# Key norms' sums behind the receptance tile and the low-rank products, the gates' small weights in program order on VectorE, two operations of each key tile on ScalarE

## The chip, the cores and the metric

The kernel runs on one core of one Trainium2 chip. The metric is the time of one execution on the device in microseconds (us). The engines are named as the profile names them: PE (matrix products), DVE (vector engine), ACT (scalar engine), POOL (GpSimd) and SP, which only issues transfers. Each engine works through its own queue in order, and waits where an instruction needs a result of another engine that isn't there yet.

## The reference, cut to what matters

One layer of a hybrid trunk on 512 frames of 1024 values, all in float32: a gated convolution, an RG-LRU and an RWKV-7 mixer, merged by gates, then an output projection and a squared-ReLU MLP.

```python
h = rms_norm(x, norm1_g)
p = h @ w_in                                   # 1024 -> 11520 columns
pa, pb, pg, pc = _split(p, (COLS_A, COLS_B, COLS_GATE, COLS_C))
y_a = b_a * causal_dwconv(c_a * x_a, conv_a_w)
y_b = rg_lru(causal_dwconv(x_b, lru_conv_w, lru_conv_b), ...) * gelu(g_b)
...
pc = token_shift(pc, rwkv_mu)                  # p + (prev - p) * mu
r, k, v, xw, xa, xg = _split(pc, (D_C, D_C, D_C, R_W, R_A, R_G))
decay = exp(-exp(-softplus(-(w0 + tanh(xw) @ w2)) - 0.5))
a = sigmoid(a0 + xa @ a2)
g_c = sigmoid(xg) @ g2
kk = heads(k * k_k)
kk = kk / maximum(sqrt(sum(kk * kk, axis=-1, keepdims=True)), 1e-12)
k = k * (1.0 + (a - 1.0) * k_a)
yc = rwkv7_recurrence(r, decay, k, v, kk, a)   # chunks of 64 frames
...
m = gate_a * y_a + gate_b * y_b + gate_c * y_c
x = x + m @ w_out
x = x + square(relu(rms_norm(x) @ mlp_w1)) @ mlp_w2
return rms_norm(x, final_g)
```

The change touches the lines of `kk` (the norm of each head's keys), `decay`, `a` and the second `k` line, and in the gates the product with `g2`.

## The kernel before

**Products.** All large products are float32 made of two parts: an operand is cast to a high part and the rest is subtracted (`hi`, `lo`), and a product takes three matmuls (`mm3`, L168 to L170). A projection tile has 128 output columns and 512 frames, so 8 x 3 = 24 matmuls of 128x512 into one PSUM bank of the pool `pp` (three banks). Its weights come by one transfer on SP (`raw`, two buffers), one cast on ACT (`whi`, L147) and one subtraction on DVE (`wlo`, L104), three buffers each. Everything smaller shares the two banks of the pool `pm`: the key sums `pn`, the low-rank products `pw` and `pa`, and the inverse's `pG` and `pT` among others.

**The key tiles.** `krv(g)` makes keys, receptance and values of group g; there are four groups and two key tiles j in each, eight in all. A key tile does this: the k projection and its token shift (`shift`, ACT L325 then DVE, gives `ks`); a square of the scaled keys on ACT (L430), split into `bh` and `bl` (L163 and L104); the sum over each head as two matmuls with a block matrix `bd` into `pn` (L433, L434); the root `rsqrt_rows`, which transposes (L194, tile `rqw`), works in 11 small steps on `rqq` and transposes back (L201); and `kk`, one DVE product of that with `ks`. Then the r projection and its shift (`rs`); the small weights `swa` (cast on ACT and subtraction on DVE, L406 and L104); `pw` (L444, L445), Tanh on ACT into `sig` (L447), plus one on DVE (L448); `pa` (L450, L451) and its Tanh into `av` (L453); the running sum of `sig` (`cum`, L455) and two Exp of it on ACT (L459, L462); and from all these the operands of the recurrence, `AR` and `BK`. There `kp` is one DVE operation with two scalars (L469, shown in the profile as L110, the line of the helper `ts2`), times `ks`. `ks`, `rs`, `kk` and the other work tiles of a key tile have one buffer each, so the next key tile's writes wait for this one's last reads.

**What runs beside them.** Of the previous group, `inverse(g-1)` inverts 64x64 triangular blocks: 31 steps of two DVE operations on tiles `dg` and `Z`, then transposes (L573, L578), 32 small matmuls `pG` (L585), and 32 more, `pT` (L595). `ab(q)` (the convolution and RG-LRU work, eight q) fills in everywhere. After the last inverse come the chain over the eight chunks with the gates beside it (`gate(q)`, small weights `swc`), the output projection and the MLP.

**What sets the order.** The code is written as generators, which `weave` runs alternately, so many steps of the filling work to one step of the critical one; a `yield` is the place where the other one may go on. A tile scheduler then orders each engine's queue by the priorities that `tc.high_priority` gives and by its own estimate of when things are ready; `tc.keep_in_program_order` holds one instruction where the program has it. The lines that the change touches are in `krv` and in `load_sw`:

```python
pn = pm.tile([P, S], F32, tag="pm", name="pn")
pe.matmul(pn, bd, sqh, start=True, stop=False)
pe.matmul(pn, bd, sql, start=False, stop=True)
kk = WP("a5")
rsqrt_rows(pk, kk, pn, 1e-24)
stt(kk, ks, pv("kk", j), kk, MUL, MUL)
```

Of the kernel before, what the change touches and what calls it, by code (L numbers as in the profile page):

```python
# [9 lines left out]
F32 = mybir.dt.float32  # L10
F32R = mybir.dt.float32r
I32 = mybir.dt.int32
AF = mybir.ActivationFunctionType
# [5 lines left out]
P = 128  # L19
# [14 lines left out]
S = 512  # L34
# [64 lines left out]
def block_kernel(ctx, tc, xt, win, par, mulr, sw, wout, w1, w2, fg, cst, eyes, out):  # L99
# [3 lines left out]
    def tt(o, a, b, op):  # L103
        return v.tensor_tensor(out=o, in0=a, in1=b, op=op)  # L104
# [9 lines left out]
    def f(t):  # L114
        return t.bitcast(F32)
# [135 lines left out]
    for i in range(2):  # L251
        load_half(wlr[1], win[CN[("lr", 1)]], i)
    gp.memset(epst[:, 0:1], EPS)
    wu = pc.tile([P, S], F32, tag="pu", name="wu")
    for i in range(NWARM):
        pe.matmul(wu, ones, zer, start=True, stop=True)
# [67 lines left out]
    def shift(pt, mu, omu, o):  # L324
        ac.activation(o, pt, AF.Copy, scale=omu)  # L325
        stt(o[:, 1:], pt[:, 0:S - 1], mu, o[:, 1:], MUL, ADD)
# [8 lines left out]
    def WP(tag, bufs=1):  # L335
        return pk.tile([P, S], F32, tag=tag, name=tag, bufs=bufs)
# [64 lines left out]
    def load_sw(pool, tag, j, a, n):  # L401
        raw = wp.tile([P, 2, P], F32, tag="swr", name="swr", bufs=2)
        sy.dma_start(raw[:, 0:n], sw[j, :, a:a + n])
        hi = pool.tile([P, n, P], F32R, tag=tag + "h", name=tag + "h", bufs=1)
        lo = pool.tile([P, n, P], F32R, tag=tag + "l", name=tag + "l", bufs=1)
        ac.copy(hi, raw[:, 0:n])  # L406
        tt(lo, raw[:, 0:n], f(hi), SUB)
        return hi, lo

    def c3(t):  # L410
# [5 lines left out]
    def krv(g, G_):  # L416
        G_.AR = pk.tile([P, 2, NC, 2, L], F32, tag="AR", name="AR")
        G_.BK = pk.tile([P, 2, NC, 2, L], F32, tag="BK", name="BK")
        vs = [p1.tile([P, S], F32, tag=f"v{h}", name=f"v{h}") for h in range(2)]
        for jj in range(2):  # L420
            j = 2 * g + jj
            rs = WP("rs")
            if j == 0:
                ks = k0
            else:
                ks = WP("ks")
                t = yield from proj(("k", j))
                shift(t, pv("mu_k", j), dvp(OMK, j), ks)
            sq = WP("a1")
            ac.activation(sq, ks, AF.Square, scale=pv("kk", j))  # L430
            sqh, sql = split(pk, sq, "b")
            pn = pm.tile([P, S], F32, tag="pm", name="pn")
            pe.matmul(pn, bd, sqh, start=True, stop=False)  # L433
            pe.matmul(pn, bd, sql, start=False, stop=True)  # L434
            kk = WP("a5")
            rsqrt_rows(pk, kk, pn, 1e-24)
            stt(kk, ks, pv("kk", j), kk, MUL, MUL)
            yield
            t = yield from proj(("r", j))
            shift(t, pv("mu_r", j), dvp(OMR, j), rs)  # L440
            yield
            swh, swl = load_sw(pk, "swa", j, 0, 2)
            pw = pm.tile([P, S], F32, tag="pm", name="pw")
            pe.matmul(pw, swh[:, 0], lws, start=True, stop=False)  # L444
            pe.matmul(pw, swl[:, 0], lws, start=False, stop=True)  # L445
            sig = WP("a1")
            ac.activation(sig, pw, AF.Tanh, bias=pv("w0", j), scale=0.5)  # L447
            v.tensor_scalar(out=sig, in0=sig, scalar1=1.0, scalar2=None, op0=ADD)  # L448
            pa = pm.tile([P, S], F32, tag="pm", name="pa")
            pe.matmul(pa, swh[:, 1], las, start=True, stop=False)  # L450
            pe.matmul(pa, swl[:, 1], las, start=False, stop=True)  # L451
            av = WP("a4")
            ac.activation(av, pa, AF.Tanh, bias=pv("a0", j), scale=0.5)  # L453
            cum = WP("a2")
            v.tensor_tensor_scan(out=cum, data0=smk, data1=sig, initial=0.0, op0=MUL, op1=ADD)  # L455
            PP = pk.tile([P, NC, L + 1], F32, tag="PPt", name="PPt")
            gp.memset(PP[:, :, 0:1], 1.0)
            Pt = PP[:, :, 1:L + 1]
            ac.activation(Pt, c3(cum), AF.Exp, scale=-0.5 * CW)  # L459
            v.tensor_copy(PL[:, g, jj], PP[:, :, L])  # L460
            pinv = WP("a3")
            ac.activation(pinv, cum, AF.Exp, scale=0.5 * CW)  # L462
            stt(G_.AR[:, jj, :, 0], c3(kk), -1.0, PP[:, :, 0:L], MUL, MUL)
            tt(G_.AR[:, jj, :, 1], c3(rs), Pt, MUL)
            t_ = WP("a1")
            stt(t_, av, 1.0, kk, ADD, MUL)
            stt(G_.BK[:, jj, :, 0], c3(t_), 0.5, c3(pinv), MUL, MUL)
            kp = WP("a2")
            ts2(kp, av, pv("ka", j), dvp(OKA, j), MUL, ADD)  # L469
            tt(kp, kp, ks, MUL)  # L470
            tt(G_.BK[:, jj, :, 1], c3(kp), c3(pinv), MUL)

            if jj == 0:
                rk = [WP(f"rk{h}") for h in range(2)]
            for h in range(2):
                r = slice(64 * h, 64 * h + 64)
                stt(rk[h][64 * jj:64 * jj + 64], rs[r], part[r, PI["rk"], j:j + 1], kp[r], MUL, MUL)

        for jj in range(2):
            for h in range(2):  # L480
                gp.dma_start(axd[:, 0:64, g, 0, 2 * h + jj].rearrange("c d t -> d c t"),
                             G_.AR[64 * h:64 * h + 64, jj, :, 0])
            gp.dma_start(rtd[:, :, g, jj].rearrange("c p t -> p c t"), G_.AR[:, jj, :, 1])
        rk = [split(pk, rk[h], ("a1", "a3") if h else "b") for h in range(2)]
        for h in range(2):
            q = 2 * g + h
            t = yield from proj(("v", q))
            shift(t, pv("mu_v", q), dvp(OMV, q), vs[h])
            yield
        for h in range(2):  # L490
            pb = pm.tile([P, S], F32, tag="pm", name="pb")
            for i in range(2):
                pe.matmul(pb, bd, rk[h][i], start=i == 0, stop=i == 1)
            BV[2 * g + h] = [bv_tile(2 * g + h, th) for th in range(2)]
            for th in range(2):
                tt(BV[2 * g + h][th], pb[:, HALF[th]], vs[h][:, HALF[th]], MUL)
        yield
        for b in range(2):
            pt = pm.tile([P, 2, 2, P], F32, tag="pm", name="pV")
            for i in range(2):  # L500
                for h in range(2):
                    pe.transpose(pt[:, i, h], vs[h][:, (2 * b + i) * P:(2 * b + i + 1) * P], ident)
            vt = p1.tile([P, 2, 2, P], F32, tag="vt", name="vt", bufs=2)
            ac.copy(vt, pt)
            for i in range(2):
                c = 2 * (2 * b + i)
                gp.dma_start(vtd[c:c + 2, :, g].rearrange("c s e v -> (c s) (e v)"),
                             vt[:, i].rearrange("p h x -> p (h x)"))
        yield
# [619 lines left out]
```

## Time and profile before

| what | us |
|---|---|
| median of three runs | 1109.31 |
| lowest and highest of them | 1108.31, 1109.75 |
| the profiled execution | 1108.38 |
| its span, first to last instruction | 1106.6 |
| PE idle in the span (1106.6 - 1056.1) | 50.5 |

The rows of the profile are read so. A group's row gives line, engine, operation, `out<-in`, shapes and count, then the busy time in us and the mean of one in ns, then the idle time of the engine just before and what ended it. A row of waits gives the engine and line that waited, the engine and line that it waited for, the total in us, the count and the longest. A row of windows gives the stretch, its length, each engine's busy us with the number of instructions (PE, then PEld, DVE, ACT and POOL where all are shown), then the clock granted to PE as a share of full speed, the DMA share and GB/s. A row of the timeline gives start and duration in us, and in brackets the idle time before it with what ended it.

By time the program falls into: the prologue (0 to 49), the key tiles with the inverses and the filling work (49 to 560), the chain with the gates (560 to 715), then output projection and MLP.

### The profile page before, as it was taken

The numbers are of one execution on the slowest core, as the hardware profiler recorded it, in microseconds if no ns is written. First come the engines' busy times: TensorE is split into PE (matmuls) and PEld (weight loads), VectorE is DVE, ScalarE is ACT, GpSimd is POOL, SyncE is SP. The second block draws the span as 40 slices with busy tenths as digits, with TensorE's granted clock in tenths as the row PEclk, the third lists the DMA queues.
The fourth block names the chain that finished last, engine by engine and source line by source line (L and its number), as shares of the span: only waits on it lengthen the run. The fifth ranks groups of instructions, "written<-read, shape, count | busy, mean of one in ns | idle before, by whom it ended". The sixth has DMA issues, their size and how long they took to land.

```text
span 1106.6 us, 16112 instructions
## 1 busy us (share of the span) xinstructions
PE 1056.1 (95%) x6396; PEld 865.3 (78%) x6396; DVE 743.6 (67%) x1276; ACT 473.9 (43%) x698; POOL 108.9 (10%) x167
## 2 busy tenths in 40 slices
PE   8899979999799989999899999999999999999996
PEld 5677868887588867887687887898888888888885
DVE  7997898879978998769947677955444443222224
ACT  6655445454344534534555444334433333221114
POOL 3211000210011101210022220001000000000001
PEclk9899989999989989999999999999999999999999
DMA  6243623562234623553279773234333335322231
GB/s 209 83 124 98 180 79 113 139 182 86 77 105 129 177 85 96 147 148 106 79 225 281 263 223 101 87 124 153 96 99 98 104 99 191 96 95 95 96 95 76
DMA packets 43324, 142.13 MB, mean 128 GB/s; under 512 B 5681, under 2 KB 9265, under 8 KB 42225
## 3 DMA queue, kind: packets, MB, share of 16 engines
q1 hardware_dynamic: 29472, 91.02, 25.7%
q0 software_dynamic: 13056, 49.03, 15.9%
q8 instruction: 50, 0.82, 0.3%
q10 hardware_dynamic: 720, 1.05, 0.3%
q14 instruction: 26, 0.20, 0.1%
HBM read 115.91 MB, written 25.17 MB: 127 GB/s over the span
## 4 chain that ended last, share of the span: by engine, by line
PE 65%; DVE 21%; DMA 5%; issue 5%; ACT 3%; POOL 1%; SPq 0%; ACTq 0%; POOLq 0%; DVEq 0%
PE pp L168 8%; PE pp L169 7%; PE pp L170 7%; PE acc L170 6%; PE acc L168 6%; PE acc L169 6%; PE p L169 5%; PE p L168 5%; PE p L170 5%; DVE wlo L104 4%; DMA raw<-in_win 3%; DVE dg L104 2%; DVE Z L104 2%; DMA rt<-rtd 1%; DVE u L107 1%
## 5 line engine op out<-in xcount | busy, mean ns | idle before, releaser
L104 DVE TENSOR_TENSOR wlo<-raw,whi 128x1024 fp32r<-128x1024 f32 (+1 forms) x164 | 199.5, 1219 | 249.8 <-ACT whi L147 248.9
L147 ACT CAST whi<-raw 128x1024 fp32r<-128x1024 f32 (+1 forms) x164 | 169.6, 1036 | 326.9 <-PE acc L170 125.1
L168 PE MATMUL pp<-hh,whi 128*128 128x512 f32 x696 | 278.5, 401 | 7.2 <-DVE ks L107 4.6
L170 PE MATMUL pp<-hh,wlo 128*128 128x512 f32 x696 | 277.5, 399 | 7.6 <-DVE wlo L104 7.6
L169 PE MATMUL pp<-hl,whi 128*128 128x512 f32 x696 | 277.4, 399 | 2.8 <-DVE hl L107 2.8
L168 PEld LDWEIGHTS pp<-hh,whi 128*128 128x128 f32 x696 | 133.7, 192 | 38.6 <-DVE ks L107 5.0
L170 PEld LDWEIGHTS pp<-hh,wlo 128*128 128x128 f32 x696 | 133.8, 192 | 37.6 <-DVE wlo L104 9.6
L169 PEld LDWEIGHTS pp<-hl,whi 128*128 128x128 f32 x696 | 133.7, 192 | 30.9 <-DVE hl L107 3.2
L170 PE MATMUL p<-h2h,wlo 128*128 128x512 f32 (+1 forms) x264 | 101.4, 384 | 0.0
L168 PE MATMUL p<-h2h,whi 128*128 128x512 f32 (+1 forms) x264 | 101.3, 384 | 0.0
L169 PE MATMUL p<-h2l,whi 128*128 128x512 f32 (+1 forms) x264 | 101.1, 383 | 0.0
L168 PE MATMUL acc<-whi,ah 128*128 128x512 f32 x256 | 99.6, 389 | 0.0
L169 PE MATMUL acc<-wlo,ah 128*128 128x512 f32 x256 | 99.6, 389 | 0.0
L170 PE MATMUL acc<-whi,al 128*128 128x512 f32 x256 | 99.6, 389 | 0.0
L168 PEld LDWEIGHTS p<-h2h,whi 128*128 128x128 f32 x264 | 49.7, 188 | 9.6
L170 PEld LDWEIGHTS p<-h2h,wlo 128*128 128x128 f32 x264 | 49.6, 188 | 9.7
L169 PEld LDWEIGHTS p<-h2l,whi 128*128 128x128 f32 x264 | 49.6, 188 | 9.5
L170 PEld LDWEIGHTS acc<-whi,al 128*128 128x128 f32 x256 | 48.0, 188 | 10.1
L169 PEld LDWEIGHTS acc<-wlo,ah 128*128 128x128 f32 x256 | 48.0, 188 | 10.0
L168 PEld LDWEIGHTS acc<-whi,ah 128*128 128x128 f32 x256 | 48.0, 188 | 9.8
L104 DVE TENSOR_TENSOR Z<-Z,dg 64x31 f32<-64x31 f32 (+15 forms) x124 | 42.2, 340 | 4.1
L104 DVE TENSOR_TENSOR dg<-Z 64x31 f32<-64x31 f32 (+15 forms) x124 | 42.2, 340 | 4.0
(296 smaller groups left out, 1457.0 us busy)
## 6 DMA issues: line engine op xcount, KB each, us to landing
raw<-in_win SPq DMA_DIRECT2D x88, 512.0 KB, 3.6
raw<-in_w SPq DMA_DIRECT2D x64, 512.0 KB, 3.5
ax<-axd POOLq DMA_DIRECT2D x8, 1024.0 KB, 7.2
axd<-AXt POOLq DMA_DIRECT2D x12, 512.0 KB, 7.2
bkd<-BKT POOLq DMA_DIRECT2D x4, 1024.0 KB, 13.6
raw<-in_wout SPq DMA_DIRECT2D x8, 512.0 KB, 4.3
bk<-bkd POOLq DMA_DIRECT2D x7, 512.0 KB, 8.0
swr<-in_sw SPq DMA_DIRECT2D x16, 128.0 KB, 2.3
```

Source lines behind the costliest of these rows:

```text
L104: return v.tensor_tensor(out=o, in0=a, in1=b, op=op)
L107: return v.scalar_tensor_tensor(out=o, in0=a, scalar=s, in1=b, op0=op0, op1=op1)
L147: ac.copy(hi[:, sl], raw[:, sl])
L168: pe.matmul(ps, wh, xh, start=start, stop=False)
L169: pe.matmul(ps, wh, xl, start=False, stop=False)
L170: pe.matmul(ps, wl, xh, start=False, stop=stop)
```

## The change

It does four things. (1) The two matmuls of `pn`, the root and `kk` move behind the r projection, its shift, `pw`, `pa` and their two Tanh; the number of `yield`s stays. (2) The one added to `sig` is an ACT operation with a bias from a new tile `one`, where it was one on DVE. (3) `kp` is an ACT operation with a scale and a bias, where it was one on DVE. (4) The DVE subtraction of the gates' small weights (`swc`) is kept in program order.

```diff
--- before.py
+++ after.py
@@ -251,6 +251,8 @@
     for i in range(2):
         load_half(wlr[1], win[CN[("lr", 1)]], i)
     gp.memset(epst[:, 0:1], EPS)
+    one = cp.tile([P, 1], F32, name="one")
+    gp.memset(one, 1.0)
     wu = pc.tile([P, S], F32, tag="pu", name="wu")
     for i in range(NWARM):
         pe.matmul(wu, ones, zer, start=True, stop=True)
@@ -404,7 +406,9 @@
         hi = pool.tile([P, n, P], F32R, tag=tag + "h", name=tag + "h", bufs=1)
         lo = pool.tile([P, n, P], F32R, tag=tag + "l", name=tag + "l", bufs=1)
         ac.copy(hi, raw[:, 0:n])
-        tt(lo, raw[:, 0:n], f(hi), SUB)
+        m = tt(lo, raw[:, 0:n], f(hi), SUB)
+        if tag == "swc":
+            tc.keep_in_program_order(m)
         return hi, lo
 
     def c3(t):
@@ -429,28 +433,28 @@
             sq = WP("a1")
             ac.activation(sq, ks, AF.Square, scale=pv("kk", j))
             sqh, sql = split(pk, sq, "b")
+            yield
+            t = yield from proj(("r", j))
+            shift(t, pv("mu_r", j), dvp(OMR, j), rs)
+            swh, swl = load_sw(pk, "swa", j, 0, 2)
+            pw = pm.tile([P, S], F32, tag="pm", name="pw")
+            pe.matmul(pw, swh[:, 0], lws, start=True, stop=False)
+            pe.matmul(pw, swl[:, 0], lws, start=False, stop=True)
+            sig = WP("a1")
+            ac.activation(sig, pw, AF.Tanh, bias=pv("w0", j), scale=0.5)
+            ac.activation(sig, sig, AF.Identity, bias=one[:, 0:1])
+            pa = pm.tile([P, S], F32, tag="pm", name="pa")
+            pe.matmul(pa, swh[:, 1], las, start=True, stop=False)
+            pe.matmul(pa, swl[:, 1], las, start=False, stop=True)
+            av = WP("a4")
+            ac.activation(av, pa, AF.Tanh, bias=pv("a0", j), scale=0.5)
+            yield
             pn = pm.tile([P, S], F32, tag="pm", name="pn")
             pe.matmul(pn, bd, sqh, start=True, stop=False)
             pe.matmul(pn, bd, sql, start=False, stop=True)
             kk = WP("a5")
             rsqrt_rows(pk, kk, pn, 1e-24)
             stt(kk, ks, pv("kk", j), kk, MUL, MUL)
-            yield
-            t = yield from proj(("r", j))
-            shift(t, pv("mu_r", j), dvp(OMR, j), rs)
-            yield
-            swh, swl = load_sw(pk, "swa", j, 0, 2)
-            pw = pm.tile([P, S], F32, tag="pm", name="pw")
-            pe.matmul(pw, swh[:, 0], lws, start=True, stop=False)
-            pe.matmul(pw, swl[:, 0], lws, start=False, stop=True)
-            sig = WP("a1")
-            ac.activation(sig, pw, AF.Tanh, bias=pv("w0", j), scale=0.5)
-            v.tensor_scalar(out=sig, in0=sig, scalar1=1.0, scalar2=None, op0=ADD)
-            pa = pm.tile([P, S], F32, tag="pm", name="pa")
-            pe.matmul(pa, swh[:, 1], las, start=True, stop=False)
-            pe.matmul(pa, swl[:, 1], las, start=False, stop=True)
-            av = WP("a4")
-            ac.activation(av, pa, AF.Tanh, bias=pv("a0", j), scale=0.5)
             cum = WP("a2")
             v.tensor_tensor_scan(out=cum, data0=smk, data1=sig, initial=0.0, op0=MUL, op1=ADD)
             PP = pk.tile([P, NC, L + 1], F32, tag="PPt", name="PPt")
@@ -466,7 +470,7 @@
             stt(t_, av, 1.0, kk, ADD, MUL)
             stt(G_.BK[:, jj, :, 0], c3(t_), 0.5, c3(pinv), MUL, MUL)
             kp = WP("a2")
-            ts2(kp, av, pv("ka", j), dvp(OKA, j), MUL, ADD)
+            ac.activation(kp, av, AF.Identity, scale=pv("ka", j), bias=dvp(OKA, j))
             tt(kp, kp, ks, MUL)
             tt(G_.BK[:, jj, :, 1], c3(kp), c3(pinv), MUL)
 
```

Line numbers of the changed kernel are 2 to 4 higher in most places; `pn` stands there at L453 and L454, `pw` at L441 and L442, `pa` at L447 and L448, the Tanh of `pw` at L444, the new addition at L445, `pG` at L589, the inverse's transposes at L577 and L582. Numbers behind a name are buffers; they differ by a few between the two kernels.

PE's queue in the third key tile (j = 2, at about 157 us). Before, `pn` stands between matmuls of the r tile (`pp_1411`) and of a tile of the filling work:

```order
L170 MATMUL pp_1411<-hh_73,wlo_1407 128x512
L168 MATMUL pp_1411<-hh_73,whi_1406 128x512
L169 MATMUL pp_1411<-hl_74,whi_1406 128x512
L433 MATMUL pn_1384<-bh_1380,bd_64 128x512
L170 MATMUL pp_1411<-hh_73,wlo_1407 128x512
L168 MATMUL pp_1425<-hh_73,whi_1420 128x512
L169 MATMUL pp_1425<-hl_74,whi_1420 128x512
L170 MATMUL pp_1425<-hh_73,wlo_1421 128x512
L434 MATMUL pn_1384<-bl_1381,bd_64 128x512
L168 MATMUL pp_1425<-hh_73,whi_1420 128x512
```

Now, in the changed kernel, 13 matmuls of the tiles named above, the four of `pw` and `pa` and 20 of other tiles stand ahead of it:

```order
L170 MATMUL pp_1515<-hh_73,wlo_1511 128x512
L168 MATMUL pp_1515<-hh_73,whi_1510 128x512
L169 MATMUL pp_1515<-hl_74,whi_1510 128x512
L170 MATMUL pp_1515<-hh_73,wlo_1511 128x512
L168 MATMUL pp_1515<-hh_73,whi_1510 128x512
L169 MATMUL pp_1515<-hl_74,whi_1510 128x512
L453 MATMUL pn_1466<-bh_1382,bd_64 128x512
L454 MATMUL pn_1466<-bl_1383,bd_64 128x512
L168 MATMUL pp_1547<-hh_73,whi_1542 128x512
L169 MATMUL pp_1547<-hl_74,whi_1542 128x512
```

The first `pn` matmul moved 37 instructions back, to behind `pw` and `pa`; `pG` of the inverse kept its place.

ACT's queue at the same place. Before, with the square (L430), its cast and the Tanh of `pw`:

```order
L430 ACTIVATE a1_1378<-ks_1288,part_66 128x512
L163 CAST bh_1380<-a1_1378 128x512
L786 ACTIVATE u5_1359<-u4_1350 128x512
L788 ACT_TABLE_LOAD
L788 ACTIVATE u2_1341<-u2_1341 128x512
L147 CAST whi_1540<-raw_1539 128x1024
L325 ACTIVATE rs_1287<-pp_1411,dv_92 128x512
L447 ACT_TABLE_LOAD
L447 ACTIVATE a1_1476<-pw_1473,part_66 128x512
L147 CAST whi_1635<-raw_1634 128x1024
L453 ACTIVATE a4_1482<-pa_1479,part_66 128x512
L797 COPY g3_1418<-pp_1425 128x512
```

Now:

```order
L434 ACTIVATE a1_1380<-ks_1290,part_66 128x512
L163 CAST bh_1382<-a1_1380 128x512
L790 ACTIVATE u5_1361<-u4_1352 128x512
L792 ACT_TABLE_LOAD
L792 ACTIVATE u2_1343<-u2_1343 128x512
L147 CAST whi_1542<-raw_1541 128x1024
L327 ACTIVATE rs_1289<-pp_1393,dv_92 128x512
L444 ACT_TABLE_LOAD
L444 ACTIVATE a1_1458<-pw_1455,part_66 128x512
L147 CAST whi_1617<-raw_1616 128x1024
L445 ACTIVATE a1_1458<-a1_1458,one_132 128x512
L450 ACTIVATE a4_1464<-pa_1461,part_66 128x512
```

The queue is the same up to the Tanh (now L444) but for the line numbers; behind it the new addition of one (L445) stands after a weight cast.

DVE's queue in the fifth key tile (j = 4, at about 282 us), where the inverse's steps (`dg` and `Z`) run with the root's (`rqw`, `rqq`). Before:

```order
L194 STREAM_TRANSPOSE rqw_2445<-pn_2441 128x512
L104 TENSOR_TENSOR dg_2082<-Z_2081 64x207
L104 TENSOR_TENSOR wlo_2567<-raw_2565,whi_2566 128x1024
L104 TENSOR_TENSOR Z_2081<-Z_2081,dg_2082 64x23x9
L197 TENSOR_SCALAR rqq_2446<-rqw_2445 128x16
L104 TENSOR_TENSOR dg_2082<-Z_2081 64x192
L110 TENSOR_SCALAR rqq_2446<-rqq_2446 128x16
L104 TENSOR_TENSOR Z_2081<-Z_2081,dg_2082 64x24x8
L104 TENSOR_TENSOR rqq_2446<-rqq_2446 128x16
L104 TENSOR_TENSOR dg_2082<-Z_2081 64x175
L107 SCALAR_TENSOR_TENSOR rqq_2446<-rqq_2446 128x16
L104 TENSOR_TENSOR Z_2081<-Z_2081,dg_2082 64x25x7
```

Now, from the same step of the inverse on:

```order
L104 TENSOR_TENSOR Z_2083<-Z_2083,dg_2084 64x22x10
L104 TENSOR_TENSOR dg_2084<-Z_2083 64x207
L104 TENSOR_TENSOR wlo_2569<-raw_2567,whi_2568 128x1024
L104 TENSOR_TENSOR Z_2083<-Z_2083,dg_2084 64x23x9
L104 TENSOR_TENSOR dg_2084<-Z_2083 64x192
L104 TENSOR_TENSOR Z_2083<-Z_2083,dg_2084 64x24x8
L104 TENSOR_TENSOR dg_2084<-Z_2083 64x175
L104 TENSOR_TENSOR Z_2083<-Z_2083,dg_2084 64x25x7
L104 TENSOR_TENSOR dg_2084<-Z_2083 64x156
L104 TENSOR_TENSOR Z_2083<-Z_2083,dg_2084 64x26x6
L104 TENSOR_TENSOR dg_2084<-Z_2083 64x135
L104 TENSOR_TENSOR Z_2083<-Z_2083,dg_2084 64x27x5
```

The root's steps are gone from between the inverse's; they stand further back, from the inverse's last steps on.

## The prediction

> **What bounds the kernel now.** I read the page's engine rows first, then the chain that ended last, then PE's waits, then the stretches round each long wait.
>
> ```profile
> span 1106.6 us, 16112 instructions
> PE 1056.1 (95%) x6396; PEld 865.3 (78%) x6396; DVE 743.6 (67%) x1276; ACT 473.9 (43%) x698; POOL 108.9 (10%) x167
> PE 65%; DVE 21%; DMA 5%; issue 5%; ACT 3%; POOL 1%; SPq 0%; ACTq 0%; POOLq 0%; DVEq 0%
> ```
>
> PE is busy 95% of the span, so only its 50.5 us of idle time, and the time that it runs at half clock behind an idle stretch, can be won. The chain gives 21% to DVE. So the question is where PE waits for DVE and ACT:
>
> ```profile
> PE pn L433 <- ACT bh L163: 9.4, 4, 5.3
> PE pp L170 <- DVE wlo L104: 7.6, 4, 5.8
> PE pp L168 <- DVE ks L107: 4.6, 1, 4.6
> PE pga L169 <- DVE ul L104: 1.8, 1, 1.8
> ```
>
> The first row is the wait that the change is about: four waits of the key sums pn for the split square, 9.4 us in all. The timeline puts the two long ones in the third and the fifth key tile (5.34 and 3.35 us); the weight wait of 5.82 us comes right behind the fifth, and the 4.6 us wait for the shift of ks is that of the seventh.
>
> ```profile
> 156.57:159.98 3.41, 0.23 (x2) 1.00 0.49 155
> 159.98:163.39 3.41, 1.24 (x3) 0.50 0.00 1
> 163.39:166.81 3.42, 3.42 (x9) 0.50 0.00 0
> 279.44:282.85 3.41, 3.41 (x8) 0.50 0.08 32
> 303.33:306.74 3.41, 1.92 (x5) 0.50 0.24 56
> 306.74:310.16 3.42, 3.42 (x56) 0.50 0.73 250
> 310.16:313.57 3.41, 3.41 (x21) 0.50 0.00 0
> ```
>
> These rows (PE busy, then the granted clock) show what a long wait costs besides itself: after a stretch of 3.41 us in which PE is almost idle the clock is 0.50, until a stretch is filled with large matmuls. Half of the working time in it is lost.
>
> **What the change takes off DVE and puts on ACT.**
>
> ```profile
> L448 DVE TENSOR_SCALAR a<-a 128x512 f32<-128x512 f32 x8 | 3.4, 419 | 0.2 <-ACT a L447 0.2
> L110 DVE TENSOR_SCALAR a<-a,part,dv 128x512 f32<-128x512 f32 x8 | 4.3, 542 | 0.0
> L447 ACT ACTIVATE a<-pw,part 128x512 f32<-128x512 f32 x8 | 5.5, 689 | 2.0 <-DVE spt L107 1.3 <-PE pw L445 0.5
> L777 ACT ACTIVATE u<-u,dv 128x512 f32<-128x512 f32 x8 | 6.6, 819 | 0.0
> L147 ACT CAST whi<-raw 128x1024 fp32r<-128x1024 f32 x160 | 167.2, 1046 | 326.9 <-PE acc L170 125.1 <-PE pp L169 104.5 <-PE p L169 56.9
> ```
>
> DVE loses 3.4 + 4.3 = 7.7 us, about 1 us a key tile. ACT gains, by the rows of the same form (one pointer 689 ns, two pointers 819 ns), 8 x 0.689 + 8 x 0.819 = 12.1 us. I cost them at nothing on the path: the weight casts, ACT's main work, sat idle 326.9 us, and that for PE. If that cover were gone and PE waited for every cast behind them, the price is 12.1 us; below nothing they can't go. The rule table of the Trainium skill (page "ScalarE: Activation LUTs", section "Rules for kernel authors") says to do add and mul on VectorE and not on ScalarE. The durations agree with it (419 and 542 ns against 689 and 819): by it the eight tiles would be 12.1 - 7.7 = 4.4 us slower, not faster. The trace speaks against that, since DVE is the engine that PE waits for and ACT is busy 43% of the span.
>
> The memset of `one` is a single one at the start, beside the loads. The order of the gates' small low halves is worth little:
>
> ```profile
> DVE swcl L104 <- ACT swch L406: 4.9, 1, 4.9
> 496.12 0.30 ACT L406 CAST swch<-swr 128x128 fp32r<-128x128 f32 x1 [6.01 <-DMA swr<-in_sw]
> 496.33 1.04 ACT L147 CAST whi<-raw 128x1024 fp32r<-128x1024 f32 x1
> ```
>
> DVE's 4.9 us of idling go away by name only: the ACT cast swch waits for its DMA in the changed order too, and the weight cast that DVE needs next stands behind it. DVE wins the 0.28 us of the one subtraction there. All the eight together I take as 0, with 1 us to either side for the changed order of the gates (560 to 690 us).
>
> **The third and fourth key tile.** In the old order PE stood at pn until the square was split. In the new order pn stands 37 instructions later, behind pw and pa, and takes its PSUM bank from pw. So it needs the Tanh of pw, and that stands in ACT's queue behind a weight cast, the shift of the r tile and a table load:
>
> ```profile
> 160.72 0.72 ACT L430 ACTIVATE a<-ks,part 128x512 f32<-128x512 f32 x1
> 165.68 0.63 ACT L788 ACTIVATE u<-u 128x512 f32<-128x512 f32 x1 [0.39 <-DVE u L107]
> 167.82 1.05 ACT L147 CAST whi<-raw 128x1024 fp32r<-128x1024 f32 x1 [1.51 <-PE pp L169]
> 168.78 0.68 ACT L325 ACTIVATE rs<-pp,dv 128x512 f32<-128x512 f32 x1
> 169.48 1.28 ACT L447 ACT_TABLE_LOAD   x1
> 170.77 0.69 ACT L447 ACTIVATE a<-pw,part 128x512 f32<-128x512 f32 x1
> 162.15 0.80 PE L433 MATMUL pn<-bh,bd 128*128 128x512 f32 x1 [5.34 <-ACT bh L163]
> 167.86 0.40 PE L444 MATMUL pw<-lws,swah 128*128 128x512 f32 x1
> 168.09 0.40 PE L445 MATMUL pw<-lws,swal 128*128 128x512 f32 x1
> 175.70 0.47 PE L585 MATMUL pG<-dg,AXt 32*32 32x32 f32 x9
> ```
>
> At full clock matmuls start 0.23 us apart (pw's two rows), at half clock 0.43. PE passes the old place of pn at 156.8, needs 13 + 4 matmuls (3.9 us) to 160.7, when the shift of ks has freed the next bank (the square starts at 160.72), and 20 more (4.6 us) to 165.3. The Tanh: the root ends at 166.3, the cast no longer waits (167.4), the shift 168.0, the table 169.3, Tanh 170.0. So a new wait of 4.7 us takes the place of 5.3. DVE's half of the r shift, which stands behind ACT's, then frees the next bank about 0.9 us later, 170.9; the rest of the half-clock stretch (to 173.6) takes 6 of the 10 matmuls ahead of pG, which starts at 174.5 instead of 175.7: 1.2 us won. The fourth tile has the same new wait without a table load, about 0.8 us. **Both: -0.4 us**, from -5 (no wait for the bank) to +2.
>
> **The fifth and sixth.** Here the gain is on DVE. The pn wait (3.35) and its half-clock stretch (3.4/2 = 1.7) go. What is late next is pG, which needs L578, the last of the inverse's transposes:
>
> ```profile
> L201 DVE STREAM_TRANSPOSE a<-rqq 128x512 f32<-128x512 f32 x8 | 5.6, 705 | 0.1
> L107 DVE SCALAR_TENSOR_TENSOR rqq<-rqq 128x16 f32<-128x16 f32 x54 | 9.3, 173 | 1.1
> 279.40 0.79 PE L433 MATMUL pn<-bh,bd 128*128 128x512 f32 x1 [3.35 <-ACT bh L163]
> 304.69 1.23 DVE L578 STREAM_TRANSPOSE dg<-Z 32x1024 f32<-32x1024 f32 x1
> 304.82 0.80 PE L170 MATMUL pp<-hh,wlo 128*128 128x512 f32 x1 [5.82 <-DVE wlo L104]
> 307.26 3.62 PE L585 MATMUL pG<-dg,AXt 32*32 32x32 f32 x64
> ```
>
> Ahead of L578 DVE no longer has: its own wait for pn (0.7), the L201 transpose and three products of 512 columns of the kk work (0.7 each, 2.8), L448 and L110 (1.0), one weight subtraction (1.2) and five small root steps (five of 173 ns, 0.2 from start to start); it has swal more (0.4). That is 6.3 us: it ends at 299.6 instead of 305.9. PE passes the old place of pn at 276.05 (279.40 less 3.35) without a wait and has 67 matmuls of 0.228 us ahead of pG, 15.3 us, and some 0.7 us of waiting for the weight subtraction between: 292.0. So it waits 7.7 us at pG, and the half clock behind it, with pG's small matmuls filling no stretch, lasts about to 306.7: (306.7 - 299.7)/2 = 3.5. Before: 3.35 + 1.7 + 5.82 + (313.6 - 304.8)/2 = 4.4, together 15.3. After: 11.2. **-4.1 us**, from -6 (L578 earlier) to -1 (one more slow stretch, and the sixth tile's pn waiting for its Tanh). What keeps the lead:
>
> ```profile
> 322.00:404.00 82.00, 81.42 (x440) 66.75 (x437) 74.76 (x136) 45.41 (x66) 10.50 (x16) 1.00 0.49 136
> 500.00:560.00 60.00, 54.39 (x307) 43.00 (x305) 55.87 (x94) 31.14 (x43) 1.13 (x2) 0.97 0.33 106
> ```
>
> From 322 to 404 PE (the second number) is the bound, 81.4 of 82 us, with DVE (the fourth) at 74.8, so what PE has won it keeps.
>
> **The seventh and eighth, and the last inverse.** The wait for the shift of ks at 403.7 stays, since the same rows stand ahead of it on DVE; it shrinks by the 1 us that DVE saved in the sixth tile. The pn of the seventh stands behind 12 matmuls and its Tanh is ready about then; the eighth's 0.47 us wait is replaced by one of the same size. **-1.0 us**, -3 to +2. In 500 to 560 the four waits (ul, wlo, and two for the u and g work) make 5.4 us and come from DVE's load, 55.9 of 60 us in the second row; I take **-0.5 us** for what the last two tiles saved.
>
> **Sum.** 0.4 + 4.1 + 1.0 + 0.5 = 6.0 us off the profiled execution's 1108.38 (span 1106.6 and 1.8 round it): 1102.4. It lies 0.9 under the median of the three runs, 1109.31; so 1103.3.
>
> **Rivals.** (1) *Everything is hidden*: no new wait for pw's bank, and pG finds its data. Then 9.4 us of waits go, and the half clock behind the two long ones, (166.8 - 162.15)/2 = 2.3 and 1.7: 13.4 in all, 1095.9. For it: bh is the only thing that the old waits name. Against it: the bank and ACT's queue above. 0.14, for 1094 to 1099.
> (2) *The waits only move*: at pG L578 comes just 4 us earlier and one more stretch is slow, and the third tile wins nothing: 1107 to 1111.5. 0.20.
> (3) *Slower, by a late kk*: the root chain now starts after the r tile and is spread over about 9 us of other DVE work; kk then frees ks, for which ACT's copy of the next key tile waits while it holds a PSUM bank. It decides if kk ends more than a projection tile (24 x 0.23 = 5.5 us) after the next key tile's last matmul. I estimate 2 to 3 us, from the root steps and subtractions above, once in each group. If it bites in two groups, each costs what the ks wait costs (4.6, and 2.3 of half clock as behind the third tile): 13.8 less the 6.0 won, 8 us slower, 1117; in one group with half of the gain gone, 6.9 - 3.0, 4 us slower: 1111.5 to 1117. 0.10.
> (4) *Slower, by late casts*: in each key tile the two new ACT operations (1.5 us) stand ahead of a weight cast. If PE waits behind all eight pairs, 12.1 us: 1115.4. Against it: the casts' 326.9 us of idle time. 0.03. This is how the rule of the Trainium skill's page "ScalarE: Activation LUTs" would come true here.
> That the change doesn't do what it says is excluded by the order.
>
> **How the numbers follow.** The forecast (1099 to 1107) has 0.53. A measurement here can tell about 0.2%, 2.2 us: faster 0.53 + 0.14 = 0.67, same 0.20, slower 0.13. The range 1097 to 1111 leaves out half of rival 1, and rivals 3 and 4.
>
> **What would show it.** Right: PE's row "pn <- ACT bh" is gone, and a wait of 4 to 5 us for the Tanh of pw stands near 165; a wait of about 7 us at pG near 292; the ks wait of 3 to 5 us near 400; DVE busy 7 to 8 us less and ACT 12 more. Wrong: no wait at the third tile's pn (rival 1), whi casts as PE's main releaser, or more waits for ks (rival 3).

## The result

| | median us | runs | lowest to highest |
|---|---|---|---|
| before | 1108.81 | 4 | 1108.03 to 1109.75 |
| changed | 1102.85 | 4 | 1100.21 to 1103.72 |

The ratio is 0.9945, 95% interval 0.9933 to 0.9958: 6.0 us faster, where the forecast was 1103.3 us with a range of 1097 to 1111. Run again later beside the kernel before, the changed kernel took 1102.99 us, ratio 0.9944 (0.9929 to 0.9959).

The page of the changed kernel, engine rows as before:

```profile
span 1101.2 us, 16113 instructions
PE 1051.8 (96%) x6396; PEld 862.7 (78%) x6396; DVE 737.7 (67%) x1260; ACT 483.9 (44%) x714; POOL 107.8 (10%) x168
```

The span lost 5.4 us. DVE is busy 5.9 us less and ACT 10.0 us more. In the stretch of the key tiles and inverses, before and then changed (its end taken at the same matmuls, 4.6 us earlier):

```profile
49.00:560.00 511.00, 482.35 (x2664) 390.94 (x2662) 442.06 (x801) 244.89 (x355) 50.94 (x79) 0.97 0.42 120
49.00:555.40 506.40, 479.77 (x2661) 389.23 (x2659) 434.98 (x785) 254.75 (x370) 50.35 (x79) 0.97 0.41 121
```

PE's idle time there fell from 511.00 - 482.35 = 28.7 to 26.6 us, 2.0 less, and its busy time by 2.6 us with the same matmuls, which is time that it no longer runs at half clock. So in this pair of profiles the waits went down little; they moved, and the slow stretches behind them shrank. How the gain splits between the two is not fixed: in the profile of the changed kernel's later run the same stretch, to the same matmul, has 24.4 us of idle time, 4.3 less than before, and its busy time is only 1.0 us less:

```profile
49.00:554.73 505.73, 481.35 (x2662) 391.05 (x2660) 434.45 (x786) 255.58 (x370) 50.51 (x79) 0.97 0.41 121
```

PE's waits in the changed kernel:

```profile
PE pG L589 <- DVE rqq L107: 7.4, 1, 7.4
PE pp L168 <- DVE ks L107: 4.6, 1, 4.6
PE pn L453 <- ACT a L444: 4.5, 1, 4.5
PE pga L169 <- DVE ul L104: 1.8, 1, 1.8
PE pp L170 <- DVE wlo L104: 1.5, 2, 1.2
PE pG L589 <- DVE u L793: 1.2, 1, 1.2
```

The row "pn <- ACT bh" (9.4 us) is gone from the top (0.7 us of it is left, in an early key tile), and the weight waits (7.6) are down to 1.5. In their place stand one wait for the Tanh of pw (L444) and one at pG. The first row names a small root step of DVE as the releaser; it is the last DVE instruction by the profile ahead of it, and the timeline shows what PE waits for, L582:

```profile
168.33 0.69 ACT L444 ACTIVATE a<-pw,part 128x512 f32<-128x512 f32 x1
169.07 0.50 PE L453 MATMUL pn<-bh,bd 128*128 128x512 f32 x1 [4.49 <-ACT a L444]
170.04 0.79 PE L168 MATMUL pp<-hh,whi 128*128 128x512 f32 x1 [0.24 <-DVE rs L107]
174.00 2.17 PE L589 MATMUL pG<-dg,AXt 32*32 32x32 f32 x63
293.37 3.84 DVE L577 STREAM_TRANSPOSE Z<-Z 32x1024 f32<-32x1024 f32 x2
297.24 1.23 DVE L582 STREAM_TRANSPOSE dg<-Z 32x1024 f32<-32x1024 f32 x1
298.62 1.56 PE L589 MATMUL pG<-dg,AXt 32*32 32x32 f32 x26 [7.45 <-DVE rqq L107]
```

L582 ends at 298.47, and pG starts 0.15 us later.

Where the lead was won is seen from the starts of the same matmuls in the two profiled executions (from the span's start, in us; `pga` is a small product of the filling work, `pA` the first product of a group's triangular blocks, `pV` the transposes of its value tiles):

| matmul | before | changed | lead |
|---|---|---|---|
| pga of the first group | 91.53 | 91.11 | 0.42 |
| second half of the pA of the second group | 226.10 | 225.42 | 0.68 |
| pga behind the fifth and sixth tile | 326.71 | 322.49 | 4.22 |
| first pA of the third group | 350.91 | 347.64 | 3.27 |
| first pA of the fourth group | 473.03 | 467.38 | 5.65 |
| pga in the last inverse | 521.10 | 514.93 | 6.17 |
| last pga | 573.58 | 568.97 | 4.61 |
| first transposes behind the output projection | 716.15 | 710.69 | 5.46 |

The first 0.4 us is the start of the program, where the change does nothing; other profiles of this study differ from the one of before by 0.2 to 1.7 us there. How far one pair of profiles can be trusted elsewhere is seen below, from second executions.

### The profile page after: what moved, and what is told of

It is laid out like the page before. It is cut to its first block, busy times and chain, and to the rows that moved or that the text cites. A ratio compares the mean times of both kernels' runs of the same rounds, so it can differ in the third digit from the quotient of the medians.

```text
span 1101.2 us, 16113 instructions
## 1 busy us (share of the span) xinstructions
PE 1051.8 (96%) x6396; PEld 862.7 (78%) x6396; DVE 737.7 (67%) x1260; ACT 483.9 (44%) x714; POOL 107.8 (10%) x168
## 4 chain that ended last, share of the span: by engine, by line
PE 67%; DVE 22%; issue 4%; ACT 3%; DMA 3%; SPq 0%; POOL 0%; ACTq 0%; DVEq 0%
PE pp L168 8%; PE pp L169 8%; PE pp L170 8%; PE acc L170 6%; PE acc L168 6%; PE acc L169 6%; PE p L170 5%; PE p L168 5%; PE p L169 5%; DVE wlo L104 4%; DVE dg L104 3%; DVE Z L104 2%; DMA raw<-in_win 2%; DVE u L107 1%; ACT whi L147 1%
```

## The experiments

"Own reference" below is the kernel before, run on the same chip in the same set (medians 1108.55, 1108.45 and 1108.73 us in the three sets); medians of different sets are compared by their ratios to it.

**The parts alone.** Each of the first three kernels is the kernel before with one part of the change, as in the diff above: part (1); parts (2) and (3); part (4).

The move alone:

> The kernel before with part (1) of the change alone: pn, the root and kk behind the r tile, pw and pa; sig's addition and kp stay on DVE, the gates' subtraction is free. Theory (the move carries the gain, because it takes the root's steps from between the inverse's steps in the fifth key tile): the waits for bh are gone, a wait of about 4.5 us for the Tanh of pw stands at the third tile, the wait at the fifth tile's pG is about 8.4 us (7.4 of the changed kernel and 1.0 for the two DVE operations that stand ahead of the transposes again), and the time is 3 to 4.5 us under that of before. Rival (DVE's 7.7 us of work carry the gain): within 1.5 us of before.

1106.47 us, ratio 0.9977 (0.9964 to 0.9989): 2.1 to 2.6 us faster, less than the 3 us and more that were expected, though the interval (1.2 to 4.0 us) doesn't exclude them. The waits are the ones expected in kind:

```profile
168.47 0.80 PE L449 MATMUL pn<-bh,bd 128*128 128x512 f32 x1 [4.49 <-ACT a L440]
300.31 1.88 PE L585 MATMUL pG<-dg,AXt 32*32 32x32 f32 x32 [7.47 <-DVE dg L578]
```

The wait at pG is 1 us shorter than expected, since PE comes to it later. So the move carries a part of the gain by itself, by the medians less than half.

The two operations on ACT alone:

> The kernel before with parts (2) and (3) alone: sig's addition and kp on ACT, pn where it was. Theory: the waits for bh stay at 8 to 10 us, the weight wait behind the fifth tile shrinks from 5.8 to 4 or 5 us, and the time is 0.5 to 2.5 us under that of before. Rival (DVE's 7.7 us carry the gain): 4 us or more under it. Rival by the rule for adds and multiplications on ACT: 2 to 4 us over it.

1105.93 us, ratio 0.9977 (0.9962 to 0.9991). The old waits are all there, those of pn and of the weights shorter:

```profile
PE pn L435 <- ACT bh L163: 7.1, 3, 3.9
PE pp L170 <- DVE wlo L104: 5.0, 2, 3.8
PE pp L168 <- DVE ks L107: 4.6, 1, 4.6
```

The sum of pn and weight waits is 12.1 us where it was 17.0; both fell a little further than expected (pn to 7.1, where 8 to 10 was expected, the longest weight wait to 3.8, where 4 or 5 was). The time, 2.6 us under its own reference, is a little better than expected too, and by the medians neither rival: DVE's work alone carries less than half of the gain, and ACT's added work didn't cost it. The interval (1.0 to 4.2 us) just touches the 4 us of the first rival.

The gates' subtraction alone:

> The kernel before with part (4) alone: the gates' subtraction in program order. The queues differ from those of before only from the last inverse on. Theory: DVE's 4.9 us of idling for the cast swch become idling for the weight cast behind it in ACT's queue, and the time is within 1 us of before. Rival (the idle time held up DVE ahead of the busiest stretch, 500 to 560): 2 us or more under it.

1108.08 us, ratio 0.9991 (0.9975 to 1.0007): no difference that can be told. DVE idles as long as before, now for the cast that stands behind swch:

```profile
496.19 1.23 DVE L104 TENSOR_TENSOR wlo<-raw,whi 128x1024 fp32r<-128x1024 f32 x1 [5.50 <-ACT whi L147]
```

The three ratios multiply to 0.9977 x 0.9977 x 0.9991 = 0.9945, the ratio of the whole. The intervals are about 0.0013 to each side, so this shows that no large part is missing, not that the parts don't touch each other.

**pn with its own bank.**

```diff
-            pn = pm.tile([P, S], F32, tag="pm", name="pn")
+            pn = pc.tile([P, S], F32, tag="pS", name="pn")
```

> The changed kernel with pn in a PSUM bank that neither pw nor pa uses (the one of pS, free in that stage). Theory (the Tanh of pw is not the last that is late; PE's next tile there needs the bank that the r shift frees on DVE at about 170): the wait for the Tanh is gone, and a wait of 4.5 to 5.5 us for DVE's rs stands a few instructions later; the time is within 1 us of the changed kernel. Rival (pw's bank is the whole wait): the wait and its half-clock stretch go, 5 to 6 us under the changed kernel.

1101.19 us, ratio 0.9935 (0.9920 to 0.9950): 1.7 us under the changed kernel by the medians, 1.1 by the ratios, whose intervals overlap. The wait for the Tanh went, but the next wait was neither that of the theory nor none. The scheduler put pn right behind pa, and PE then waited for both halves of the square:

```profile
160.84 0.49 PE L453 MATMUL pn<-bh,bd 128*128 128x512 f32 x1 [1.64 <-ACT bh L163]
162.68 0.79 PE L454 MATMUL pn<-bl,bd 128*128 128x512 f32 x1 [1.34 <-DVE bl L104]
168.24 0.72 DVE L107 SCALAR_TENSOR_TENSOR rs<-pp,part,rs 128x511 f32<-128x511 f32 x1
```

Together 3.0 us in place of 4.5, and with the slow clock behind them PE came to the bank of rs no earlier than rs was done. So in this place several operands come one behind another within 9 us, and taking one wait away uncovers the next. The bank is not the only thing that changed here: pn also stands 20 matmuls further forward.

**pG further back.** `NINV` is 7, and `g == 1` is the inverse beside the fifth and sixth key tile.

```diff
-        for _ in range(NINV):
+        for _ in range(18 if g == 1 else NINV):
             yield CPI
```

> The changed kernel with pG of the fifth tile 50 instructions (11.4 us of matmuls) further back in PE's queue. Theory (DVE is the bound there, and pG is only the place where PE meets it): the wait of 7.4 us leaves pG and a wait of 6 to 7.5 us for a weight subtraction, which stands behind the same transposes in DVE's queue, takes its place; within 1 us of the changed kernel. Rival (pG stands too early in PE's queue and other work could cover it): the wait and its half-clock stretch go, 8 to 10 us under the changed kernel.

1099.56 us, ratio 0.9920 (0.9906 to 0.9935). The mechanism is the expected one:

```profile
297.34 1.23 DVE L582 STREAM_TRANSPOSE dg<-Z 32x1024 f32<-32x1024 f32 x1
299.16 1.21 DVE L104 TENSOR_TENSOR wlo<-raw,whi 128x1024 fp32r<-128x1024 f32 x1
300.42 0.80 PE L170 MATMUL pp<-hh,wlo 128*128 128x512 f32 x1 [5.92 <-DVE wlo L104]
```

The wait left pG and stands at a weight subtraction behind the same transposes. But the time was not within 1 us: it fell by about 3 us. PE met the wait later (at 294.5, where it was 291.2), and the wait itself is 1.5 us shorter. When it ends PE has done ten matmuls more (2.3 us at full clock), but it ends 1.8 us later, so 0.5 us is won by that. The rest is the clock. In the changed kernel pG's small matmuls are the first behind the wait, and three stretches run at half clock (296.07 to 306.31); here large matmuls are the first, and there are two (297.65 to 304.47). The last slow stretch of the changed kernel, and the one at the same place here:

```profile
302.90:306.31 3.41, 3.41 (x10) 0.50 0.17 61
304.43:307.84 3.41, 3.41 (x16) 0.99 0.13 53
```

From the wait's end that is 7.7 us at half clock against 4.1, half of the difference 1.8 us; with the 0.5 it makes 2.3, and from the second group's pA to the third's this profile is 2.5 us shorter than that of the changed kernel. DVE is the bound in this place, but what PE has done before it waits, and which matmuls stand right behind, still counts.

**The k tile's bank read by ACT alone.**

```diff
-                shift(t, pv("mu_k", j), dvp(OMK, j), ks)
+                sq = WP("a1")
+                ac.activation(ks, t, AF.Copy, scale=dvp(OMK, j))
+                ac.activation(sq, t, AF.Copy, scale=pv("mu_k", j))
+                tt(ks[:, 1:], sq[:, 0:S - 1], ks[:, 1:], ADD)
```

> The changed kernel with both reads of the k tile's PSUM bank on ACT (0.7 us more of ACT work a key tile), so that DVE's half of the shift no longer holds the bank. Theory (DVE is the bound near 400 too, since the next tile's weight subtraction stands just ahead of that shift): the 4.6 us wait for ks becomes one of 3 to 3.6 us for a weight subtraction; 0.5 to 1.5 us under the changed kernel. Rival (the bank alone holds PE): the wait goes with its half-clock stretch, 5.5 to 7 us under it.

1102.40 us, ratio 0.9942 (0.9926 to 0.9959). In its profile the wait near 400 is the next row of DVE's queue, as expected:

```profile
404.74 0.80 PE L170 MATMUL pp<-hh,wlo 128*128 128x512 f32 x1 [3.05 <-DVE wlo L104]
```

The time that this gives, 0.5 us in the medians, is too small to tell from none.

**ACT's new work doubled.**

```diff
             ac.activation(sig, sig, AF.Identity, bias=one[:, 0:1])
+            ac.copy(sig, sig)
...
             ac.activation(kp, av, AF.Identity, scale=pv("ka", j), bias=dvp(OKA, j))
+            ac.copy(kp, kp)
```

> The changed kernel with an ACT copy more behind each of the two operations that it put on ACT (16 copies of 0.58 to 0.62 us, 9.6 us of ACT work, which change no value). Theory (ACT's work there is hidden; it has waited for PE or DVE before each): at most 1.5 us over the changed kernel, and no weight cast becomes PE's main releaser. Rival (casts late behind the new ACT work): 5 to 10 us over it.

1104.77 us, ratio 0.9970 (0.9960 to 0.9981): 2 to 3 us over the changed kernel, more than the theory's 1.5 and under the rival's 5. The profiled execution is the slowest of its ten (1108.61 us), 3.8 us over their median, so its profile shows more loss than the median has. It puts 1.0 us in the key tiles (the last pga stands at 569.96 where it was 568.97), for these 9.9 us:

```profile
L446 ACT COPY a<-a 128x512 f32<-128x512 f32 x8 | 5.0, 627 | 0.1
L475 ACT COPY a<-a 128x512 f32<-128x512 f32 x8 | 4.9, 618 | 0.2
586.59 1.65 PE L658 MATMUL py<-St,rt 64*64 64x64 f32 x32 [1.51 <-DMA rt<-rtd]
```

No wait for a weight cast came up, beyond the 0.2 us behind the chain that the kernel before has too. The rest of the loss in that profile, 4.7 us, lies between 569 and 591, in waits at the start of the chain of chunks (the third row is one), where these copies don't run. A wait of 1.50 us for rt stands there in the second profile of the changed kernel too, without these copies, so that row comes and goes between executions of one kernel. What the copies have to do with the rest stays open.

**Both, and all three edits.**

> The changed kernel with both edits, pn in pS's bank and the k tile's bank read by ACT alone. Theory: they act in different places and add up: 2 to 3.5 us under the changed kernel, 1099 to 1101. Rival (DVE's queue takes back behind the one what was won at the other): no better than the better of the two.

1097.92 us, ratio 0.9907 (0.9892 to 0.9921): 4 us and more under the changed kernel, outside the expected 1099 to 1101. By the medians that is more than the two gave alone, 1.1 to 1.7 and 0.5 us; the intervals are too wide to call it shown.

> The changed kernel with the three edits of the earlier runs: pn in pS's bank, the k tile's bank read by ACT alone, the fifth tile's pG 50 instructions further back. Theory: the first two add up to 4 to 5 us and pG's place to 2 more, as they act in different places (157 to 170, 400 to 412, 290 to 320): 1095 to 1097. Rival (with PE earlier at the fifth tile, DVE's queue takes all of the third edit back): 1097.5 to 1099, as without it.

1096.45 us, ratio 0.9889 (0.9869 to 0.9910), the best of the study: 12.3 us under its own reference, and 6.5 us under the changed kernel in the same set (1102.99). It is faster than both kernels.

> The same with the fifth tile's pG 14 instructions further back in place of 50. Theory (what the 50 won is that PE reaches the next late weight subtraction with more matmuls done): PE then meets pG again, with a wait of 3.5 to 5 us after 14 matmuls (3.2 us) more; between the run with both other edits and the one with 50: 1096 to 1098.

1098.58 us, ratio 0.9911 (0.9887 to 0.9935). PE did not meet pG again: the wait is the one for the weight subtraction, and as long as with 50 instructions. First the row with 50, then the one with 14:

```profile
298.50 0.80 PE L170 MATMUL pp<-hh,wlo 128*128 128x512 f32 x1 [5.94 <-DVE wlo L104]
296.57 0.79 PE L170 MATMUL pp<-hh,wlo 128*128 128x512 f32 x1 [5.94 <-DVE wlo L104]
```

So the expectation fell: 14 instructions are enough to get past pG. What the other 36 give beyond that is not told apart by these runs, since the two intervals overlap; nor do the 14 show a gain over the kernel with the first two edits alone (0.9907). In their profiles pG's matmuls start 2.0 us behind that wait with 14 instructions (298.57) and 11.0 us behind it with 50 (309.46), and the half clock lasts 13.7 us in the one (293.74 to 307.38) and 6.8 in the other (295.13 to 301.95).

> The changed kernel once more, beside these two on one chip: 1101.5 to 1104, a ratio of 0.993 to 0.996 to the kernel before.

1102.99 us, ratio 0.9944, inside what was expected.

## Why the prediction was right, point by point

The terms below are read from one pair of profiles, and two executions of one program differ too. The program with the gates' subtraction alone has PE's queue of before up to 636 us and DVE's up to 490, so its profile is a second execution of before for the key tiles. The changed kernel was profiled twice. The times between the matmuls of the table above, in us:

| from, to | before | gates alone | move alone | two ACT operations alone | changed | changed again |
|---|---|---|---|---|---|---|
| pga of the first group, pA of the second | 134.57 | 134.96 | 135.69 | 133.67 | 134.31 | 133.20 |
| pga behind the fifth and sixth tile | 100.61 | 101.04 | 97.33 | 99.60 | 97.07 | 97.18 |
| pA of the third group | 24.20 | 24.20 | 25.42 | 24.24 | 25.15 | 25.18 |
| pA of the fourth group | 122.13 | 120.89 | 121.04 | 120.98 | 119.75 | 119.72 |
| pga in the last inverse | 48.07 | | 48.10 | 47.51 | 47.55 | 47.54 |
| last pga | 52.48 | | 53.53 | 52.51 | 54.03 | 54.12 |
| py that waits for rt | 14.47 | | 13.32 | 13.42 | 13.34 | 14.55 |

The first, fourth and last rows differ by 1.1 to 1.2 us between two executions of one program, and a term of that size can't be read from one pair. The gain in the second row is 3.4 to 4.0 us in any pair, and the move alone gives almost all of it; the loss in the third row comes with the move.

**The third and fourth tile** (-0.4 forecast): the lead went from 0.42 to 0.68, -0.3; with the other executions it is -0.3 to -1.8. The new wait was forecast at 4.7 us for the Tanh of pw and measured at 4.49 (3.46 in the second profile); pG was forecast at 174.5 and stands at 174.00 (0.4 us of that from the program's start). That pw's bank is the reason was shown by the kernel with the bank of its own: there that wait is gone.

**The fifth and sixth** (-4.1 forecast): -3.5. L582 was forecast to end at 299.6 and ended at 298.47, and PE's wait at pG was forecast at 7.7 us and measured at 7.45. So the claim that the old wait's place on PE would be taken by the inverse's transposes held, and the kernel with pG further back showed that DVE is what is late there. What the forecast did not see is that 1.0 us of the lead was lost again between 326 and 351; it said that PE keeps there what it has won. The value tiles' transposes now wait (0.27 us before), which is 0.6 of it:

```profile
344.40 0.55 PE L506 MATMUL pV<-ident,v 128*128 128x128 f32 x3 [0.89 <-DVE v L107]
```

**The seventh and eighth** (-1.0 forecast): -2.4 (3.27 to 5.65) in this pair of profiles and -1.1 against the second execution of before, by another way than forecast. The step that failed is that the ks wait "shrinks by the 1 us that DVE saved in the sixth tile". It is 4.59 us before and 4.64 after, and 4.58 to 4.64 in the six other kernels that leave the k tile's shift as it was. DVE's timeline in the changed kernel says why:

```profile
395.97 0.06 DVE L793 MEMSET u<- 128x1 f32 x1 [0.55 <-ACT u L792]
397.34 1.22 DVE L796 TENSOR_TENSOR_SCAN u<-u,u 128x512 f32<-128x512 f32 x1
402.70 1.23 DVE L104 TENSOR_TENSOR wlo<-raw,whi 128x1024 fp32r<-128x1024 f32 x1
404.26 0.75 DVE L107 SCALAR_TENSOR_TENSOR ks<-pp,part,ks 128x511 f32<-128x511 f32 x1
405.06 0.61 PE L168 MATMUL pp<-hh,whi 128*128 128x512 f32 x1 [4.64 <-DVE ks L107]
```

DVE was idle at 395.97, waiting for ACT's root. So it carried no backlog there that a saving could shorten; from that moment the same rows stand ahead of ks. The kernel before has the same idle row, and the same 9.1 us from it to the end of PE's wait:

```profile
399.21 0.06 DVE L789 MEMSET u<- 128x1 f32 x1 [0.55 <-ACT u L788]
408.31 0.80 PE L168 MATMUL pp<-hh,whi 128*128 128x512 f32 x1 [4.59 <-DVE ks L107]
```

The second step, "the eighth's 0.47 us wait is replaced by one of the same size", failed to the good side: the wait went, and so did a half-clock stretch behind it. In windows of PE alone, before:

```profile
436.46:439.87 3.41, 3.41 (x69) 1.00 0.22 82
439.87:443.28 3.41, 3.41 (x9) 0.50 0.38 74
```

and in the changed kernel, where pn no longer stands beside the two runs of small pT (16 matmuls each in the program, 32 records each in the trace):

```profile
429.37:432.78 3.41, 3.41 (x48) 1.00 0.91 268
432.78:436.20 3.42, 3.42 (x42) 1.00 0.09 23
436.20:439.60 3.40, 3.40 (x17) 1.00 0.65 139
```

That is 1.7 + 0.47 us of the 2.4. But the 1.7 can't be put down to the change: the second execution of before has the same queue and the same times there (its wait is 0.34) without the slow stretch (the last section has the rows). So about half of the 2.4 us is luck of the profile of before. That the rest, 1.1 to 1.2 us, is near the forecast -1.0 is luck too, since the wait that was to give it didn't shrink; neither the move alone nor the ACT operations alone show it, and what gives it stays open.

**500 to 560** (-0.5 forecast): 1.0 us lost up to the last pga (5.65 to 4.61), and 1.1 won back right behind it, up to the chunks (PE's wait at the first py that needs rt was 1.54 us and is 0.45). That 1.1 us is no gain of the change: the second profile of the changed kernel has 1.50 us there. The 0.5 us that the forecast wanted from DVE's savings shows earlier, between the pA of the fourth group and the last inverse (5.65 to 6.17), in both profiles and with the ACT operations alone. Waits did shrink (5.4 us in four; now 1.8, 1.2 and 1.2), but two stretches at half clock took the place of one; the last section has one of them.

**The gates and the small operations.** "No cost for ACT's work" held in kind: 726 and 813 ns a piece (forecast 689 and 819), 10.0 us more of ACT, and no weight cast among PE's waits in the key tiles. The forecast signs of 12 us more of ACT and 7 to 8 less of DVE (5.9) were not met by the engine rows; by rows of instructions ACT's two new ones are 5.8 + 6.5 = 12.3 us and DVE's two old ones 3.4 + 4.3 = 7.7 are gone, but other rows of DVE became longer: the inverse's first transposes from 15.9 to 16.4 us, two of the root's steps from 1.5 and 1.4 to 2.2 and 2.1. The gates' order at 0 held: 0.9991 with an interval that takes in 1.

**The rivals.** The first, that everything is hidden, fell with the two new waits of 4.49 and 7.45 us. The second, that the waits only move, is half true of the waits (2.0 and 4.3 us less idle time in the two profiles), but L582 came more than 4 us earlier and the time lies under its 1107. Against the third, a late kk, stands the ks row: one wait of 4.6 us, as before. Against the fourth stands that no weight cast holds PE in the key tiles.

So the sum was right because its largest term was (4.1 against 3.5 here, and 3.4 to 4.0 in any pair), and because what it had wrong elsewhere is small: 1.0 us lost between 326 and 351 that it did not count, and the terms of the seventh and eighth tile and of 500 to 560, which came by other ways or not at all. In this pair of profiles an error of 1.4 us to the fast side in the eighth tile cancelled them, and that was luck. That the medians differ by just the 6.0 us of the forecast is luck as well: the pair of profiles gives 5.0 us from the first pga on. That the ratio of the parts alone is 0.9977 for the move and 0.9977 for the two ACT operations was no part of the forecast, which didn't split them; the expectation for the move alone was too high.

## What to carry to other kernels

A wait that is taken away gives what lies between it and the next operand that is late; look for that one in the queues of the engine that delivers it, bank reuse included, before counting the wait as won. Before a term of about 1 us is read from a pair of profiles, profile the same program twice. A saving on a busy engine shortens a later wait only if that engine has no idle time in between: read its timeline back from the wait to its last idle row. Edits in different places that gave 0.5, 1.7 and 3.3 us alone by the medians gave 6.5 together, a little more than they add up to.

## What was not expected of the hardware

A stretch that is full of small matmuls did not bring the clock back here: before the change, 306.74 to 310.16 was busy throughout with 56 instructions, most of them 32x32, and the next stretch still ran at 0.50 (the prediction's rows). Nor did it keep the clock: before, 436.46 to 439.87 was busy throughout with 69 instructions, 64 of them pT, and the next stretch ran at 0.50.

And whether the clock drops depends on where the stretches fall. In one execution all the slow ones behind the first start and end a whole number of 3.413 us apart, in each profile of this study (before, from 439.87 to 549.10 it is 32 of them), but from execution to execution this grid lies elsewhere. Before, an edge lies at 439.87. In the profile of the gates' subtraction alone the grid of its slow stretch (406.11 to 412.94) has an edge at 440.24, and PE's matmuls there start within 0.03 us of the same times. The clock stayed:

```profile
436.83:440.24 3.41, 3.41 (x62) 1.00 0.13 46
440.24:443.66 3.42, 3.42 (x17) 1.00 0.48 93
```

With waits it looks alike. The wait for ul in the last inverse is 1.80 us before and 1.76 us in the changed kernel. Before, an edge at 521.79 cuts it; in the changed kernel it lies whole between two edges. The two stretches before, then the two changed:

```profile
518.38:521.79 3.41, 3.12 (x14) 1.00 0.06 23
521.79:525.20 3.41, 1.90 (x8) 1.00 0.49 156
514.53:517.94 3.41, 1.65 (x8) 1.00 0.22 61
517.94:521.35 3.41, 3.41 (x10) 0.50 0.23 93
```

Beside itself the same wait cost nothing in the one and half of 3.4 us in the other. A forecast by sums can't say which of the two a short wait will get, and that is worth 1 to 2 us a wait here.
